# Logits of the stick-breaking attention: the queries' high by the keys' low parts as 64-row products, two query tiles issued as a pair

## The chip, the core and the metric

The kernel runs on one core of a Trainium2 chip. The metric is the device time of one execution in microseconds (us). The core has a matrix engine (TensorE, PE in the profile, whose weight loads are listed apart as PEld), a vector engine (DVE), a scalar engine (ACT), a general engine (POOL) and a queue that issues transfers (SP).

## What is computed

One layer of a gated encoder block: a combined input projection, an attention branch with 8 heads of 64 channels, a spatial gating branch, two up projections with gates, an output projection and a final norm. The change lies in the first line of the attention below.

```
def stick_breaking_attention(q, k, v):           # 1024 positions, 8 heads, 64 channels
    for start in range(0, s, Q_BLOCK):           # Q_BLOCK = 128
        z = einsum('bhqd,bhkd->bhqk', qb, kb)    # logits
        before = s_idx < t_idx
        log_keep = where(before, log_sigmoid(-z), 0.0)
        log_stick = cumsum(log_keep, reverse=True) - log_keep
        w = where(before, exp(log_sigmoid(z) + log_stick), 0.0)
        outs.append(einsum('bhqk,bhkd->bhqd', w, vb))
```

## The kernel before

Every float32 product is made of rounded parts: a value is split into a high part and a low part (`hi_lo`), both of type fp32r, and the products of the parts are added up in PSUM. The projections leave keys and queries of two heads at a time in DRAM, as `kq_hi[p]` and `kq_lo[p]`.

**One head.** `load_head(p, h)` brings four tiles of the tag `k` (6 buffers) to SBUF. A head has 64 channels and the array 128 rows, so `q` holds the high part of the queries in rows 0 to 63 and the low part in rows 64 to 127, while `kh` holds the keys' high part twice, one copy under the other, and `kl` the keys' low part twice. One product of `q` with `kh` over 128 rows is then high by high plus low by high, and one of `q` with `kl` is high by low plus low by low. `v` holds the values.

**One query tile.** `attn_row` works on 128 queries (tile `i`) by up to 512 keys (half `c`): both products go into one PSUM bank of the tag `z` (2 buffers), then ACT reads the bank twice (`keep` and `beta`, two sigmoids), a scan on DVE follows, and a product on DVE or POOL gives the weights. On the diagonal the tile is 128, 256, 384 or 512 keys wide, elsewhere 512. `attn_step` calls it for four tiles, transposes the weights on PE (bank `tr`) and multiplies them with the values (bank `o`). A head has 12 such query tiles, and 8 heads have 96: 16 each of 128, 256 and 384 keys, and 48 of 512.

**What sets the order.** The code doesn't issue anything itself. Each helper (`mm`, `act`, `load`, ...) records a task with an engine and a cost, and `Plan.issue` plays them through as a list scheduler: whenever an engine is free, it starts the recorded task with the lowest number of those that are ready and whose buffers can be had; a task that needs a buffer which is still held is passed over, and the next one in number is taken. `can_start` gives the buffers of a tag out in the order in which they were recorded. The program that results has a fixed order on each engine. The work of the projections (banks X, Y and Z) is recorded around the heads, and so stands between the products of the attention on PE.

```
for item in skipped:            # passed over: a buffer is held
    heapq.heappush(heap, item)
```

Of the kernel before, what the change touches and what calls it, by code (L numbers as in the profile page):

```python
# [10 lines left out]
F32 = mybir.dt.float32  # L11
F32R = mybir.dt.float32r
# [4 lines left out]
P = 128  # L17
S = 1024
# [72 lines left out]
class Plan:  # L91
# [10 lines left out]
    def buf(self, tag, shape=(P, 512), dt=F32):  # L102
        return Buf(self, tag, shape, dt)
# [22 lines left out]
        self.tasks.append(t)  # L126


    def mm(self, out, lhsT, rhs, start, stop, **kw):
        self.add("PE", max(0.109, rhs.n * 0.000417 + 0.0135) * (2 if rhs.buf.dt == F32 else 1),  # L130
                 lambda: self.nc.tensor.matmul(out.ap(), lhsT=lhsT.ap(), rhs=rhs.ap(), start=start, stop=stop, **kw),  # L131
                 [out], [lhsT, rhs])

# [200 lines left out]
def hybrid_block(  # L334
# [37 lines left out]
    pl = Plan(tc, make_tile, slots, psum_tags)  # L372
    buf = pl.buf
# [22 lines left out]
    def half_of(half):  # L396
        return slice(half * 512, half * 512 + 512)
# [201 lines left out]
    kq_hi = [buf("d", (2, P, S)) for _ in range(4)]  # L599
    kq_lo = [buf("d", (2, P, S)) for _ in range(4)]  # L600
# [33 lines left out]

    def load_head(p, h):
        hs = slice(64 * h, 64 * h + 64)
        kh, kl, q, v = (buf("k", (P, S), F32R), buf("k", (P, S), F32R), buf("k", (P, S), F32R),
                        buf("k", (P, 8, P), F32R))
        for side in range(2):
            pl.load(kh[64 * side:64 * side + 64, :], kq_hi[p][0, hs, :])  # L640
        pl.load(q[0:64, :], kq_hi[p][1, hs, :])
        pl.load(q[64:128, :], kq_lo[p][1, hs, :])
        for side in range(2):
            pl.load(kl[64 * side:64 * side + 64, :], kq_lo[p][0, hs, :])
        pl.load(v.all, v_all[:, :, 2 * p + h, :].map(lambda a: a.rearrange("b p c -> p b c")))
        return kh, kl, q, v
# [4 lines left out]
    nc.vector.memset(first_one.ap(), 0.0)  # L651
    nc.vector.tensor_copy(first_one.ap()[:, 384:512], ident.ap())

    def attn_row(kh, kl, q, i, c, cr):

        diag = i // 4 == c
        w = (i % 4 + 1) * P if diag else 512
        z = buf("z")[:, 0:w]
        qs, ks = q[:, i * P:(i + 1) * P], slice(512 * c, 512 * c + w)
        pl.mm(z, qs, kh[:, ks], True, False)  # L660
        pl.mm(z, qs, kl[:, ks], False, True)
        keep, beta = buf("ak", (P, 544)), buf("r")
        pl.act(keep[:, 0:w], z, AF.Sigmoid, scale=-0.125)
        pl.act(beta[:, 0:w], z, AF.Sigmoid, scale=0.125)
        edge = keep[:, w:w + 1]
        kr = keep[:, 0:w].map(lambda a: a[:, ::-1])
        if diag:
            pl.add("POOL", 0.15, lambda: nc.gpsimd.memset(edge.ap(), 0.0), [edge], [])
            pl.scan(kr, kr, first_one[:, 512 - w:512].map(lambda a: a[:, ::-1]), 0.0)
            if c == 1:  # L670
                pl.copy(cr, keep[:, 0:1])
        else:
            pl.copy(edge, cr)
            pl.scan_mult(kr, kr, cr)
        pl.tt(beta[:, 0:w], beta[:, 0:w], keep[:, 1:w + 1], ALU.mult, eng="DVE" if diag else "POOL")
        return beta

    def attn_step(kh, kl, q, v, p, h, ch, os_):
        o = buf("o")
        first = True  # L680
        for c in range(ch, -1, -1):
            crs = [carry[:, 8 * (2 * p + h) + ii:8 * (2 * p + h) + ii + 1] for ii in range(4)]
            w = [attn_row(kh, kl, q, 4 * ch + ii, c, crs[ii]) for ii in range(4)]
            for j in range(4):
                i0 = j if c == ch else 0
                off = i0 * P
                tr = buf("tr")
                for ii in range(i0, 4):
                    pl.transpose(tr[:, ii * P:(ii + 1) * P], w[ii][:, j * P:(j + 1) * P], ident)
                wh, wl = buf("e", dt=F32R), buf("e", dt=F32R)  # L690
                pl.hi_lo(wh[:, off:512], wl[:, off:512], tr[:, off:512])
                va = v[:, 4 * c + j, :]
                pl.mm(o[:, off:512], va, wh[:, off:512], first, False)
                pl.mm(o[:, off:512], va, wl[:, off:512], False, c == 0 and j == 3)
                first = False
        mine, other = slice(64 * h, 64 * h + 64), slice(64 - 64 * h, 128 - 64 * h)
        pl.copy(os_[mine, :], o[other, :])
        pl.tt(os_[mine, :], o[mine, :], os_[mine, :], ALU.add)
        if h == 1:
            g = buf("f1")  # L700
            pl.load(g.all, za[p][:, half_of(ch)])
            pl.tt(os_.all, os_.all, g.all, ALU.mult, eng="POOL")
            if p < 3:
                pl.store(y_a[p][:, half_of(ch)], os_.all)
# [119 lines left out]
    def head(p, h):  # L824
        parts = load_head(p, h)
        for ch in range(2):
            if h == 0:
                sums_of[p, ch] = buf("os")
            attn_step(*parts, p, h, ch, sums_of[p, ch])
# [4 lines left out]
    for word in ORDER.split():  # L834
        name = word.strip("+0123456789")
        n = int(word[-1])
# [115 lines left out]
    for c in range(2):  # L952
        for a in range(2):
            t = buf("T", (P, 4, 512))
# [81 lines left out]
```

## Time and profile before

| | |
|---|---|
| median of 3 runs | 761.28 us (761.17 to 762.08) |
| profiled execution, its own time | 762.38 us |
| its span, first to last instruction | 760.5 us |
| PE busy | 734.5 us, 97% |
| PEld busy | 607.9 us, 80% |
| DVE, ACT, POOL busy | 563.3, 432.2, 304.4 us |

Times in the rows are microseconds unless marked ns. A product on PE has two records, the load of its weights (PEld) and the product itself. Products follow one another before the record of the one ahead has ended, so what one costs on the engine is the distance from its start to the next one's start, not the length of its record; in a row that merges several of a kind, the first starts at the time shown, and the last ends at that time plus the length. L131 is the line of the helper `mm`, through which all products go, L135 that of the transposes; they are told apart by their tiles. `k,k` are the logits (a tile of keys and the tile of queries), `T,b` the projections, `e,k` the weights by values, `c,r` the transposes of the weights. A clock of 1.00 is the upper of the two levels of TensorE's clock, 2.4 GHz.

### The profile page before, as it was taken

To read this page: it belongs to the slowest core of one execution; us is meant where nothing else is said; L and a number is where in the kernel's file an instruction comes from. 1 tells how busy PE (TensorE), PEld (TensorE's weight loads), DVE (VectorE), ACT (ScalarE), POOL (GpSimd) and SP (SyncE) were. 2 spreads that over 40 slices of the span, in tenths; PEclk is the share of its full clock that TensorE was granted. 3 is DMA by queue.
4 is the path that set the end of the run, shared out by engine and by line. 5 is a ranking of instruction groups with operands and counts; after the bars stand their busy time and mean duration, and the time that the engine had idled before them with its cause. 6 is when DMAs were issued, how large, how long until landed. Compare 5 with 4: busy or idle time off the path is not lost.

```text
span 760.5 us, 10807 instructions
## 1 busy us (share of the span) xinstructions
PE 734.5 (97%) x3524; PEld 607.9 (80%) x3524; DVE 563.3 (74%) x788; ACT 432.2 (57%) x920; POOL 304.4 (40%) x298
## 2 busy tenths in 40 slices
PE   4998999999999999999999999999999999999996
PEld 3876888888888888878888788888888878888885
DVE  4769544688858877888979888798888999961132
ACT  6645754655746556657677585767856555431122
POOL 1400364598647963561655535260321140013110
PEclk9999999999999999999999999999999999999999
DMA  9513259633344554453656336464697837880022
GB/s 343 183 42 109 72 179 250 204 87 137 104 152 129 173 206 142 116 172 112 170 162 179 99 99 192 125 153 153 220 318 232 239 112 230 258 300 2 28 83 111
DMA packets 69177, 121.31 MB, mean 160 GB/s; under 512 B 7296, under 2 KB 17024, under 8 KB 69120
## 3 DMA queue, kind: packets, MB, share of 16 engines
q1 hardware_dynamic: 67968, 118.52, 50.1%
q10 hardware_dynamic: 1152, 2.10, 0.7%
q8 instruction: 28, 0.46, 0.2%
q14 instruction: 29, 0.24, 0.1%
HBM read 81.27 MB, written 39.32 MB: 159 GB/s over the span
## 4 chain that ended last, share of the span: by engine, by line
PE 85%; DVE 4%; issue 4%; DMA 2%; POOL 2%; ACT 1%; SPq 0%; POOLq 0%; DVEq 0%
PE Y L131 22%; PE X L131 22%; PE Z L131 19%; PE z L131 9%; PE o L131 8%; PE tr L135 5%; DVE T L168 1%; DMA k<-d 1%; DVE ak L192 1%; DMA k<-in_x_dram 1%; POOL a L168 1%; POOL r L168 1%; DMA f<-d 1%; DVE b L168 0%; POOL b L168 0%
## 5 line engine op out<-in xcount | busy, mean ns | idle before, releaser
L131 PE MATMUL Y<-T,b 128*128 128x512 f32 x672 | 182.7, 400 | 2.8 <-ACT b L159 2.0
L131 PE MATMUL X<-T,b 128*128 128x512 f32 x660 | 176.1, 397 | 0.0
L159 ACT CAST b<-a 128x512 fp32r<-128x512 f32 (+1 forms) x152 | 93.3, 616 | 103.3 <-PE X L131 25.1
L131 PE MATMUL Z<-T,b 128*128 128x512 f32 x540 | 145.2, 397 | 0.0
L131 PEld LDWEIGHTS Y<-T,b 128*128 128x128 f32 x672 | 123.0, 189 | 26.8 <-ACT b L159 2.4
L131 PEld LDWEIGHTS X<-T,b 128*128 128x128 f32 x660 | 120.7, 188 | 22.9 <-ACT Y L159 0.3
L168 DVE TENSOR_TENSOR b<-a,b 128x512 fp32r<-128x512 f32 (+1 forms) x112 | 100.2, 896 | 47.3 <-ACT b L159 42.1
L131 PEld LDWEIGHTS Z<-T,b 128*128 128x128 f32 x540 | 98.7, 189 | 18.9
L168 POOL TENSOR_TENSOR b<-a,b 128x512 fp32r<-128x512 f32 x40 | 58.3, 1457 | 104.4 <-ACT b L159 97.3
L168 POOL TENSOR_TENSOR f<-f,f 128x512 f32<-128x512 f32 (+1 forms) x38 | 59.1, 1563 | 37.3 <-ACT f L148 17.7
L168 POOL TENSOR_TENSOR a<-a,a 128x512 f32<-128x512 f32 x40 | 60.9, 1523 | 26.2 <-DVE b L168 21.5
L168 POOL TENSOR_TENSOR r<-r,ak 128x512 f32<-128x512 f32 x32 | 46.6, 1466 | 54.7 <-DVE ak L192 46.0
L199 DVE TENSOR_TENSOR_SCAN ak<-ak,c 128x128 f32<-128x128 f32 (+1 forms) x64 | 63.2, 990 | 4.2 <-ACT ak L148 4.0
L131 PE MATMUL o<-e,k 128*128 128x512 f32 (+1 forms) x192 | 59.6, 343 | 1.6 <-DVE e L168 1.5
L168 DVE TENSOR_TENSOR e<-tr,e 128x512 fp32r<-128x512 f32 (+1 forms) x96 | 52.1, 546 | 11.9 <-ACT e L159 11.3
L131 PE MATMUL z<-k,k 128*128 128x512 f32 (+2 forms) x216 | 60.2, 355 | 0.2 <-DMA k<-d 0.2
L135 PE MATMUL tr<-c,r 128*128 128x128 f32 x320 | 58.7, 273 | 1.0 <-POOL r L168 1.0
L148 ACT ACTIVATE ak<-z 128x128 f32<-128x128 f32 (+2 forms) x96 | 47.2, 494 | 20.1 <-PE z L131 14.5
L159 ACT CAST e<-tr 128x512 fp32r<-128x512 f32 (+1 forms) x96 | 45.7, 479 | 22.3 <-PE tr L135 19.7
L148 ACT ACTIVATE r<-z 128x128 f32<-128x128 f32 (+2 forms) x96 | 47.1, 494 | 14.3 <-PE tr L135 13.9
L192 DVE TENSOR_TENSOR_SCAN ak<-ak,c 128x512 f32<-128x512 f32 x32 | 50.6, 1594 | 0.0
L135 PEld LDWEIGHTS tr<-c,r 128*128 128x128 f32 x320 | 40.6, 140 | 12.3 <-POOL r L168 1.8
(217 smaller groups left out, 1144.9 us busy)
## 6 DMA issues: line engine op xcount, KB each, us to landing
d<-f SPq DMA_DIRECT2D x112, 256.0 KB, 2.8
a<-in_w_pairs_dram SPq DMA_DIRECT2D x80, 256.0 KB, 2.7
f<-d SPq DMA_DIRECT2D x72, 256.0 KB, 3.6
k<-d SPq DMA_DIRECT2D x48, 256.0 KB, 5.4
k<-in_x_dram SPq DMA_DIRECT2D x8, 512.0 KB, 7.2
d<-b SPq DMA_DIRECT2D x16, 256.0 KB, 2.3
k<-d SPq DMA_DIRECT2D x8, 512.0 KB, 6.9
a<-in_w_up_dram SPq DMA_DIRECT2D x16, 256.0 KB, 3.9
```

The lines of the kernel that those rows point to most:

```text
L131: lambda: self.nc.tensor.matmul(out.ap(), lhsT=lhsT.ap(), rhs=rhs.ap(), start=start, stop=stop, **kw),
L135: self.add("PE", 0.109, lambda: self.nc.tensor.transpose(out=out.ap(), in_=in_.ap(), identity=ident.ap()), [out], [in_, ident])
L148: return self.nc.scalar.activation(out=out.ap(), in_=in_.ap(), func=func, scale=sc, **kw)
L159: lambda: self.nc.scalar.copy(out=out.ap(), in_=in_.ap()), [out], [in_])
L168: self.add(eng, cost, lambda: e.tensor_tensor(out=out.ap(), in0=in0.ap(), in1=in1.ap(), op=op), [out], [in0, in1])
L192: lambda: self.nc.vector.tensor_tensor_scan(out.ap(), in_.ap(), in_.ap(), 1.0 if init is None else init.ap(), op0=ALU.mult, op1=ALU.bypass),
L199: lambda: self.nc.vector.tensor_tensor_scan(out.ap(), in_.ap(), floor.ap(), init, op0=ALU.mult, op1=ALU.max), [out], [in_, floor])
```

## The change

The products of `q` with `kl` are made over 64 rows of the array in place of 128: only the high part of the queries is multiplied with the low part of the keys, and low by low is left out. The query tiles are taken in pairs. In the odd tile of a pair the two parts of `q` are swapped, so that its high part lies in rows 64 to 127, and the product of the even tile uses rows 0 to 63, that of the odd tile rows 64 to 127. `logits` records, for a pair: even by `kh`, odd by `kh`, odd by `kl`, even by `kl`; the last has a planning cost of 0.03 us. `attn_row` no longer makes the products, and takes a bank.

To swap the parts, `q` gets the shape (128, 4, 2, 128) and is loaded by four transfers of 64 rows by 4 by 128 elements (pieces of 512 bytes), where there were two of 64 rows by 1024 elements (pieces of 4 KB).

```
-    def mm(self, out, lhsT, rhs, start, stop, **kw):
+    def mm(self, out, lhsT, rhs, start, stop, beside=False, **kw):
-        self.add("PE", max(0.109, rhs.n * 0.000417 + 0.0135) * (2 if rhs.buf.dt == F32 else 1),
+        self.add("PE", 0.03 if beside else max(0.109, rhs.n * 0.000417 + 0.0135) * (2 if rhs.buf.dt == F32 else 1),
...
-        kh, kl, q, v = (buf("k", (P, S), F32R), buf("k", (P, S), F32R), buf("k", (P, S), F32R),
+        kh, kl, q, v = (buf("k", (P, S), F32R), buf("k", (P, S), F32R), buf("k", (P, 4, 2, P), F32R),
...
-        pl.load(q[0:64, :], kq_hi[p][1, hs, :])
-        pl.load(q[64:128, :], kq_lo[p][1, hs, :])
+        for odd in range(2):
+            for side in range(2):
+                src = (kq_hi, kq_lo)[odd ^ side][p][1, hs, :]
+                pl.load(q[64 * side:64 * side + 64, :, odd, :],
+                        src.map(lambda a, odd=odd: a.rearrange("p (n t c) -> p n t c", t=2, c=P)[:, :, odd, :]))
...
+    def logits(kh, kl, q, i, c):
+        zs = []
+        for k in range(2):
+            w = ((i + k) % 4 + 1) * P if i // 4 == c else 512
+            zs.append(buf("z"))
+            pl.mm(zs[k][:, 0:w], q[:, i // 2, k, :], kh[:, 512 * c:512 * c + w], True, False)
+        for k in (1, 0):
+            w = ((i + k) % 4 + 1) * P if i // 4 == c else 512
+            rows = slice(64 * k, 64 * k + 64)
+            pl.mm(zs[k][:, 0:w], q[rows, i // 2, k, :], kl[rows, 512 * c:512 * c + w], False, True, beside=k == 0)
+        return zs
...
-        z = buf("z")[:, 0:w]
-        qs, ks = q[:, i * P:(i + 1) * P], slice(512 * c, 512 * c + w)
-        pl.mm(z, qs, kh[:, ks], True, False)
-        pl.mm(z, qs, kl[:, ks], False, True)
+        z = z[:, 0:w]
...
-            w = [attn_row(kh, kl, q, 4 * ch + ii, c, crs[ii]) for ii in range(4)]
+            w = []
+            for i2 in (0, 2):
+                zs = logits(kh, kl, q, 4 * ch + i2, c)
+                w += [attn_row(zs[k], 4 * ch + i2 + k, c, crs[i2 + k]) for k in range(2)]
```

What the planner makes of it on PE, in the second half of the first head's work. The names are: `z` the bank, `k_1089` the tile `kh`, `k_1111` the tile `q`, `k_1124` (after: `k_1125`) the tile `kl`; the size is that of the result, 128 queries by so many keys. Before:

```order
L131 MATMUL z_2942<-k_1089,k_1111 128x384
L131 MATMUL z_2942<-k_1124,k_1111 128x384
L131 MATMUL Y_2695<-T_684,b_2808 128x512
L131 MATMUL Y_2695<-T_704,b_2808 128x512
L131 MATMUL Y_2695<-T_684,b_2826 128x512
L131 MATMUL Y_2695<-T_684,b_2808 128x512
L131 MATMUL Y_2695<-T_704,b_2808 128x512
L135 MATMUL tr_2893<-c_66,r_2898 128x128
L135 MATMUL tr_2917<-c_66,r_2898 128x128
L131 MATMUL z_2965<-k_1089,k_1111 128x512
L131 MATMUL z_2965<-k_1124,k_1111 128x512
```

The same two query tiles, which are one pair, after:

```order
L132 MATMUL z_2952<-k_1089,k_1111 128x384
L132 MATMUL z_2952<-k_1125,k_1111 128x384
L132 MATMUL Y_2699<-T_684,b_2812 128x512
L132 MATMUL Y_2699<-T_704,b_2812 128x512
L132 MATMUL Y_2699<-T_684,b_2830 128x512
L132 MATMUL Y_2699<-T_684,b_2812 128x512
L132 MATMUL z_2963<-k_1089,k_1111 128x512
L132 MATMUL z_2963<-k_1125,k_1111 128x512
```

Each product with `kl` still stands right behind the product with `kh` of its own bank, and four products of a projection stand between the two tiles of the pair.

The place in the last head where two tiles of a pair come closest after the change (`k_5956` is `kh`, `k_6214` is `q`, `k_6387` is `kl`):

```order
L132 MATMUL z_6657<-k_5956,k_6214 128x512
L132 MATMUL z_6657<-k_6387,k_6214 128x512
L132 MATMUL z_6664<-k_5956,k_6214 128x512
L132 MATMUL z_6664<-k_6387,k_6214 128x512
L132 MATMUL o_6670<-e_6661,k_6417 128x512
```

Here too a product over 128 rows, the odd tile's with `kh`, stands between the two products over 64 rows.

On SP, the loads of the first head's `q` (`k_1111`) and `kl`, before:

```order
L224 DMA k_1089<-d_977 64x1024 x2
L224 DMA k_1111<-d_977 64x1024
L224 DMA a_1119<-in_w_spatial_dram 128x256
L224 DMA k_1124<-d_992 64x1024
L224 DMA k_1111<-d_992 64x1024
L224 DMA k_1124<-d_992 64x1024
```

and after:

```order
L225 DMA k_1089<-d_977 64x1024 x2
L225 DMA k_1111<-d_977 64x4x128 x2
L225 DMA a_1120<-in_w_spatial_dram 128x256
L225 DMA k_1125<-d_992 64x1024
L225 DMA k_1111<-d_992 64x4x128 x2
L225 DMA k_1125<-d_992 64x1024
```

The two transfers have become four, at the same place in the queue.

## Rows read from the trace of the kernel before

**Rows 1.** The page: busy time of each engine, and the granted clock in 40 slices.
```profile
PE 734.5 (97%) x3524; PEld 607.9 (80%) x3524; DVE 563.3 (74%) x788; ACT 432.2 (57%) x920; POOL 304.4 (40%) x298
PEclk9999999999999999999999999999999999999999
```

**Rows 2.** The page: the chain of work that ended last, by engine.
```profile
PE 85%; DVE 4%; issue 4%; DMA 2%; POOL 2%; ACT 1%; SPq 0%; POOLq 0%; DVEq 0%
```

**Rows 3.** Busy time by engine in the stretch of the heads (length, engines, clock, transfers).
```profile
core 0: us, PE busy (x) PEld busy (x) DVE busy (x) ACT busy (x) POOL busy (x), PEclk, DMA share, GB/s
288.00:618.00 330.00, 327.20 (x1640) 271.22 (x1639) 287.29 (x387) 220.18 (x517) 125.64 (x144) 1.00 0.58 171
```

**Rows 4.** Waits of PE in 285 to 625 us: total, times, longest.
```profile
PE o L131 <- DVE e L168: 1.5, 2, 1.1
PE tr L135 <- POOL r L168: 1.0, 2, 0.6
PE z L131 <- DMA k<-d: 0.2, 1, 0.2
```

**Rows 5.** Groups by line and form, PE and PEld: busy us, mean ns of one.
```profile
L131 PE MATMUL X<-T,b 128*128 128x512 f32 x660 | 176.1, 397 | 0.0
L131 PE MATMUL z<-k,k 128*128 128x512 f32 x120 | 38.4, 400 | 0.0
L131 PE MATMUL z<-k,k 128*128 128x384 f32 x32 | 8.2, 337 | 0.0
L131 PE MATMUL z<-k,k 128*128 128x128 f32 x32 | 6.9, 261 | 0.2 <-DMA k<-d 0.2
L131 PEld LDWEIGHTS z<-k,k 128*128 128x128 f32 x216 | 39.3, 188 | 7.7 <-DMA k<-d 0.6
```

**Rows 6.** PE in order of time, the first head: start, length, count.
```profile
288.55 0.60 PE L135 MATMUL z<-c,ak 128*128 128x128 f32 x4
288.91 0.42 PE L131 MATMUL z<-k,k 128*128 128x128 f32 x2
289.16 0.69 PE L131 MATMUL X<-T,b 128*128 128x512 f32 x2
...
292.22 0.51 PE L131 MATMUL z<-k,k 128*128 128x384 f32 x2
292.57 0.62 PE L131 MATMUL Y<-T,b 128*128 128x512 f32 x2
...
301.08 0.62 PE L131 MATMUL z<-k,k 128*128 128x512 f32 x2
301.53 1.07 PE L131 MATMUL X<-T,b 128*128 128x512 f32 x4
302.44 0.38 PE L135 MATMUL tr<-c,r 128*128 128x128 f32 x2
302.58 1.87 PE L131 MATMUL X<-T,b 128*128 128x512 f32 x7
304.29 0.39 PE L131 MATMUL o<-e,k 128*128 128x512 f32 x1
...
319.25 0.22 PE L131 MATMUL z<-k,k 128*128 128x128 f32 x1
319.31 2.51 PE L131 MATMUL Z<-T,b 128*128 128x512 f32 x10
```

**Rows 7.** The page: transfers into the tag k, KB each, median us to landing.
```profile
k<-d SPq DMA_DIRECT2D x48, 256.0 KB, 5.4
k<-d SPq DMA_DIRECT2D x8, 512.0 KB, 6.9
```

**Rows 8.** SP in order of time, loads of the third head.
```profile
346.16 1.09 SPq L224 DMA_DIRECT2D k<-d  x2
349.77 0.33 SPq L224 DMA_DIRECT2D a<-in_w_pairs_dram  x1
365.06 1.72 SPq L224 DMA_DIRECT2D k<-d  x3
```

**Rows 9.** PE in order of time, the third head's first product of logits.
```profile
367.37 0.22 PE L131 MATMUL z<-k,k 128*128 128x128 f32 x1
```

More of the change, by code (lines that the diff above doesn't have):

```diff
@@ L652, in hybrid_block, with attn_row @@
     nc.vector.tensor_copy(first_one.ap()[:, 384:512], ident.ap())
-    def attn_row(kh, kl, q, i, c, cr):
+    def logits(kh, kl, q, i, c):
[9 more added lines that the diff above has]
+        return zs
+    def attn_row(z, i, c, cr):
         diag = i // 4 == c
         w = (i % 4 + 1) * P if diag else 512
-        z = buf("z")[:, 0:w]
-        qs, ks = q[:, i * P:(i + 1) * P], slice(512 * c, 512 * c + w)
-        pl.mm(z, qs, kh[:, ks], True, False)
-        pl.mm(z, qs, kl[:, ks], False, True)
+        z = z[:, 0:w]
         keep, beta = buf("ak", (P, 544)), buf("r")
```

## The prediction

> **What bounds the kernel now.** I read the page's busy times and clock first, then the chain, then the stretch in which the heads are worked on, then who makes PE wait there, and last the single products. PE is busy 734.5 us of a span of 760.5, at a clock that stands at its upper level in every slice [rows 1], and 85% of the chain that ended last runs over PE [rows 2]. In the stretch of the heads, from 288 to 618 us, it is busy 327.20 of 330.00 us, and DVE, the next one, 287.29 [rows 3]. Between 285 and 625 us PE waited 2.7 us in all, of which 0.2 for the tiles that the change loads in another way [rows 4]. So in this stretch a microsecond more or less on PE is a microsecond of the whole. DVE has 43 us of room before it would become the bound.
>
> What a product costs PE is the distance between starts. The two products of a bank with 512 keys and what follows start at 301.08 and 301.53: 0.225 us each; with 384 keys 292.22 to 292.57, 0.175 each; a product of 128 keys between others 0.06 (319.25 to 319.31) [rows 6]. The record of a product of 512 lasts 0.397 us [rows 5], so it has a tail of about 0.17 us, in which the next one already runs.
>
> **What it would save, and what the order says of that.** The change wants the two products over 64 rows of a pair to run at the same time. There are 48 pairs: 16 of 128 beside 256 keys, 16 of 384 beside 512, 16 of 512 beside 512. If the narrower one vanished wholly, that would be 16 x (0.06 + 0.175 + 0.225) = 7.4 us, 1% of the time. But the order that the planner gives the changed program doesn't hold one such pair. Of the 96 products over 64 rows, none is next to another one. Each follows the product with `kh` of its own bank, or stands alone, and behind it comes a product over 128 rows. The reason is in the planner: the two banks `z` come free one after the other, since ACT has to read a bank twice before it is free. When the first one is free, the even tile's `kh` product starts, the odd tile's can't have its bank yet, and the lowest task that can run is the even tile's product with `kl`. Even where two tiles of a pair follow directly on one another, `kh` of the odd one lies between. PE executes this fixed order, so that the gain of 7.4 us can't arise; this is known before a run.
>
> The Trainium skill says in "TensorE: Matmul & The Clock Gate", Part 3, that products on different row groups run at the same time, a few nanoseconds apart. By it the pairs would give about what I worked out as the gain, if they were pairs; a product over 64 rows between two over 128 shares no time with either, as these use all rows.
>
> **What the change leaves and adds on PE.** The number of products and their columns stay: 3524 products, 96 of them now over 64 rows with the same 128 weights per row and the same up to 512 columns. Leaving out low by low takes rows, not columns, from the product, so I count nothing for it. New is that the array changes from 128 rows to 64 and back 96 times: 192 changes. The trace has no product over 64 rows, so it doesn't show their price; I bound it by neighbouring rows.
> - Lower end: nothing. The nearest change of kind in the trace is between products and transposes. Two transposes start at 302.44, seven products of 512 from 302.58, and the next one at 304.29 [rows 6]: 1.85 us, of which seven times 0.225 are 1.58, and two transposes at 0.11 (four at 288.55 in 0.60, a record being about 0.27) are 0.22. So 0.05 us is left for two changes of kind, 0.025 each. But there all 128 rows stay in use. A price below nothing I exclude: a product over 64 rows has the same number of columns, and neighbours over 128 rows leave it nothing to run beside.
> - Upper end: nothing of the next product may begin before the record of the one ahead has ended, and then its weights are loaded first: 0.397 + 0.188 - 0.225 = 0.36 us for a change [rows 5, 6]; 192 x 0.36 = 69 us.
> - Between: only the products themselves wait for one another, the weights are loaded beforehand. Then a change costs at most the tail, 0.17 us, and 192 x 0.17 = 33 us. It would be less if reading the next operand and writing the last result can lie over one another. Another row on a stall of this kind is the two products of 128 keys at 288.91, behind four transposes: with what follows at 289.16, 0.125 us each in place of 0.06, because weights are not loaded fast enough behind such short products [rows 6]; 0.065 each is what a partly hidden load costs.
>
> I take half of the tail, 0.08 us, which is near this last row: the last columns have to leave the array, but the read ahead and the write behind still overlap. 192 x 0.08 = 15.4 us.
>
> The Trainium skill has a rule that speaks against this change: "TensorEngine Tiling (Array Packing)", Tiling Modes, Key Properties, says that changing the tiling mode, and not only the tile, drains the engine. No row here shows it, and the page gives no price. An estimate by "TensorE: Matmul & The Clock Gate", Part 2, where the array drains in about 128 cycles: at 2.4 GHz that is 0.053 us, so 192 changes would be 10 us and the time 771.
>
> **The transfers.** `q` takes four transfers in place of two, 16 more in all, and of 512-byte pieces, 1024 for each head. The tile `v` is already loaded in 1024 such pieces: it lands 6.9 us after issue, where the other loads of the tag take 5.4 [rows 7]. SP's issue of two took 1.09 us [rows 8], so that 16 more are about 9 us on a queue that PE doesn't wait for. The cover: for the third head, the pair of loads at 346.16 is `q`, and the first product of that head starts at 367.37 [rows 8, 9], 21 us later; the four pieces need some 2.2 us of issue and 7 to land. The loads of `kl` stand behind them, but start 19 us later (365.06), when buffers come free. So I count nothing. If the cover were gone, a head would wait up to 1.5 us longer for its first product, 12 us over 8 heads; but PE has other products to do there.
>
> **The order otherwise.** Line by line the programs are similar: the same products, shifted by a few places against the projections. PE's own waits are 2.7 us in the stretch [rows 4], so that there is at most that to win, and I allow 3 us the other way. I count 0.
>
> **The sum.** The profiled execution took 762.4 us (span 760.5), 1.1 over the median of the runs. 762.4 + 15.4 = 777.8, and against the median 776.7. I predict 777 us.
>
> **The rivals.**
> - *Changing between 128 and 64 rows costs nothing.* Then only order and transfers are left, and the time is 759 to 764. For it: the change to transposes and back costs 0.025 us or less [rows 6]. Against it: there the array's division into rows stays the same, here sums have to leave it at another place. This is the rival on the other side, not slower; it decides if a change costs under 0.008 us (192 x 0.008 = 1.5 us). Chance 0.27.
> - *Weights wait too.* A product over other rows can't have its weights loaded while the one ahead runs. A change then costs 0.17 to 0.36 us, and the time is 794 to 830. For it: PEld is busy 607.9 us beside PE's 734.5 [rows 1], the kernel lives on loads that lie under products, and a load of 0.188 us that comes out from under a product of 0.225 nearly doubles it. Against it: it takes both costs at every one of 192 changes. Chance 0.25.
> - *The pairs do run side by side.* That would be 754. The order excludes it: chance 0.
>
> **How the numbers follow.** The forecast, a price of 0.03 to 0.17 us for a change, has 0.48 and gives 767 to 794. What a measurement of this kernel can tell from no change is about 0.2%, 1.5 us. Forecast and the second rival are slower throughout, 0.73; the first rival, spread over its range by the order's 3 us, gives faster 0.07, same 0.16, slower 0.04. So faster 0.07, same 0.16, slower 0.77. For the range I take the first rival whole (from 759), the forecast, and the second rival up to 812 (0.265 us for a change); what is left out is a good third of that rival, about 0.1, and some 0.05 below.
>
> **What the profile after would show.** Each step: the group of logits products splits in two, 96 over 64 rows; the number of PE's instructions stays 3524; the distance from a product over 64 rows to the next, and from the one ahead to it, is 0.03 to 0.17 us longer than 0.225; PE's busy time in the stretch of the heads grows by about 15 us, as the stretch itself does; the weight loads behind a change show whether they began before the product ahead ended (forecast) or after (second rival); no product over 64 rows starts within 0.1 us of another one. PE's waits for `k` stay under 1 us. I am wrong if the distances are 0.225 as before, if the stretch grows without them (then it is order or transfers), or if they are over 0.4.

## The result: slower by 5%, and the profile after

The changed kernel takes 801.64 us (801.54 to 801.72), the kernel before beside it 761.6 us: a ratio of 1.0514, 95% interval 1.0497 to 1.0531, 40 us more. The profiled execution has a span of 799.9 us, where it had 760.5.

The page after, busy times and clock, answers to [rows 1], and the chain to [rows 2]:

```profile
PE 773.6 (97%) x3524; PEld 609.7 (76%) x3524; DVE 560.5 (70%) x788; ACT 434.9 (54%) x920; POOL 299.5 (37%) x298
PEclk9999999999999999999999999999999998999998
...
PE 93%; DVE 2%; issue 2%; ACT 1%; DMA 1%; POOL 1%; SPq 0%; POOLq 0%; DVEq 0%; ACTq 0%
```

PE has the same 3524 products and is busy 39 us longer; the other engines do what they did. The weight loads take as long in sum (609.7 us, 607.9 before), so the loads as a whole did not get slower by themselves.

The groups of logits products by form (columns: busy us, mean ns of one, idle before), which answer to [rows 5]: the 64-row products have longer records than those over 128 rows, by 57 ns (128 keys) to 85 ns (512 keys).

```profile
L132 PE MATMUL z<-k,k 128*128 128x512 f32 x72 | 26.3, 411 | 0.0
L132 PE MATMUL z<-k,k 64*128 64x512 f32 x48 | 23.8, 496 | 0.0
L132 PE MATMUL z<-k,k 128*128 128x128 f32 x16 | 4.3, 267 | 0.0
L132 PE MATMUL z<-k,k 64*128 64x128 f32 x16 | 5.2, 324 | 0.0
```

Waits of the weight loads between 285 and 660 us (total us, times, longest) that the profile calls "issue", because it shows nothing that was waited for. The trace of before has none of them in its heads:

```profile
PEld z L132 <- issue: 26.3, 89, 0.4
PEld Z L132 <- issue: 4.5, 20, 0.2
PEld X L132 <- issue: 3.7, 16, 0.2
```

The second place where time went is the end of the last head. Busy time by engine in stretches around it:

```profile
core 0: us, PE busy (x) PEld busy (x) DVE busy (x) ACT busy (x) POOL busy (x), PEclk, DMA share, GB/s
288.00:630.00 342.00, 342.00 (x1544) 257.19 (x1543) 265.81 (x353) 206.74 (x474) 117.33 (x135) 1.00 0.53 160
...
645.00:662.00 17.00, 13.23 (x52) 7.93 (x51) 16.56 (x24) 13.38 (x37) 6.71 (x5) 0.92 0.05 16
662.00:670.00 8.00, 8.00 (x35) 6.71 (x34) 5.67 (x10) 1.80 (x3) 1.97 (x2) 0.75 0.16 57
```

From 288 to 630 us PE is busy all the time; before it was 327.20 of 330.00 [rows 3]. From 645 to 662 us it is busy 13.23 of 17 us, DVE 16.56: here DVE sets the pace. The granted clock falls within this stretch (0.92) and is 0.75 in the next one, so a part of each ran at the lower level, 1.2 GHz.

Set product against product by their number on PE, the changed kernel is 30.8 us late at the 2875th product (by then 89 of the 96 products over 64 rows have run), and 39.6 us at the 3125th, 63 us later; from there on nothing is added. So about 31 us come evenly over the heads and some 9 at the end of the last one.

### The profile page after: what moved, and what is told of

It is laid out like the page before. It is cut to its first block, busy times and chain, and to the rows that moved or that the text cites. A ratio compares the mean times of both kernels' runs of the same rounds, so it can differ in the third digit from the quotient of the medians.

```text
span 799.9 us, 10821 instructions
## 1 busy us (share of the span) xinstructions
PE 773.6 (97%) x3524; PEld 609.7 (76%) x3524; DVE 560.5 (70%) x788; ACT 434.9 (54%) x920; POOL 299.5 (37%) x298
## 4 chain that ended last, share of the span: by engine, by line
PE 93%; DVE 2%; issue 2%; ACT 1%; DMA 1%; POOL 1%; SPq 0%; POOLq 0%; DVEq 0%; ACTq 0%
PE Y L132 24%; PE X L132 23%; PE Z L132 20%; PE z L132 11%; PE o L132 9%; PE tr L136 5%; DMA k<-in_x_dram 1%; DVE T L169 1%; DVE ak L200 1%; PE z L136 0%; ACT T L160 0%; DVE f L169 0%; ACT ak L149 0%; POOL r L169 0%; POOL os L169 0%
## 5 line engine op out<-in xcount | busy, mean ns | idle before, releaser
L132 PE MATMUL Y<-T,b 128*128 128x512 f32 x672 | 184.7, 405 | 2.8 <-ACT b L160 2.0
L132 PE MATMUL z<-k,k 128*128 128x512 f32 (+2 forms) x216 | 76.6, 399 | 0.0
L169 POOL TENSOR_TENSOR f<-f,f 128x512 f32<-128x512 f32 (+1 forms) x38 | 56.0, 1483 | 35.1 <-ACT f L149 19.3
L132 PEld LDWEIGHTS z<-k,k 128*128 128x128 f32 x216 | 40.2, 186 | 32.0 <-issue 26.3
```

Source lines behind the costliest of these rows:

```text
L169: self.add(eng, cost, lambda: e.tensor_tensor(out=out.ap(), in0=in0.ap(), in1=in1.ap(), op=op), [out], [in0, in1])
```

## Experiments

**The rows alone.** The kernel before in its own order, engine by engine; only the 96 products with `kl` use 64 rows.

```
-        pl.mm(z, qs, kl[:, ks], False, True)
+        pl.mm(z, qs, kl[:, ks], False, True, rows=slice(0, 64))
```

`mm` then takes `lhsT.ap()[rows]` and `rhs.ap()[rows]`, while the planner sees whole tiles.

> The kernel before, in the same order on every engine and with its own loads; only the 96 products of q with kl use rows 0 to 63 in place of all 128, which leaves low by low out. Changes between 128 and 64 rows: 184. Theory 1, the price is at the change (the trace after gives 40 us over 192 changes, 0.21 us each): 184 x 0.21 = 39 us, about 800 us. Theory 2, the price comes from the new order, the pairs' hold on two banks and the loads in small pieces: about 762 us.

Measured: 792.8 us, ratio 1.0396 (1.0381 to 1.0412), 30.6 us more. This is theory 1 in kind, with 0.166 us for each of 184 changes in place of 0.21; theory 2 falls as the main cause. As the order is that of the kernel before, the same products can be laid side by side. PE of this kernel at the two products of the bank that start at 301.08 in [rows 6], and the weight loads of the same stretch:

```profile
304.11 0.82 PE L131 MATMUL z<-k,k 128*128 128x512 f32 x2
304.86 1.19 PE L131 MATMUL X<-T,b 128*128 128x512 f32 x4
305.89 0.38 PE L135 MATMUL tr<-c,r 128*128 128x128 f32 x2
...
303.89 0.19 PEld L131 LDWEIGHTS z<-k,k 128*128 128x128 f32 x1
304.44 0.18 PEld L131 LDWEIGHTS z<-k,k 64*128 64x128 f32 x1 [0.36 <-issue]
304.86 0.76 PEld L131 LDWEIGHTS X<-T,b 128*128 128x128 f32 x4 [0.24 <-issue]
```

In the trace of before the weight loads of that stretch are:

```profile
300.85 0.42 PEld L131 LDWEIGHTS z<-k,k 128*128 128x128 f32 x2
301.31 0.87 PEld L131 LDWEIGHTS X<-T,b 128*128 128x128 f32 x4
```

From the first product's start to the transposes 1.78 us pass (304.11 to 305.89), where 1.36 passed (301.08 to 302.44): 0.42 more for one product between two changes. Before, the second load began with the first product (300.85 + 0.42 - 0.19 = 301.08). Now it begins 0.33 us after the start of the product ahead (304.44), 0.1 later than that product's 0.225 us of columns, and the load behind it comes another 0.42 later (304.86). At each of the two changes 0.1 us passes in this way before the load begins; about 0.11 us more is lost at each, which I take for the part of the load of 0.18 us that the product has to wait for. This split is argued: the records of a load and of its product start together at a change. At none of the 184 changes in this trace does the load begin within the columns of the product ahead, so none is made in advance over a change of rows. Taken over all 96 places (start of the `kh` product to the start of the third one behind it, this kernel less the one before), the loss is 0.40 us for 512 keys, 0.39 for 384, 0.35 for 256 and 0.27 for 128, where the weights had been late already; together 35.1 us, of which 0.8 is counted twice where two of these places overlap. The 34.3 us left, 0.186 for a change, are what the changes cost on PE. Another 3.7 us PE got back outside of these places, nearly all of it at six where PE or its weight loads had waited for DVE or POOL in the kernel before, the largest just behind the stretch of [rows 4] (total us, times, longest):

```profile
PE Z L131 <- DVE T L168: 1.3, 1, 1.3
```

Of this wait 1.2 us are gone in the kernel with 64 rows.

**The order and the loads alone.** The changed kernel, in its own order on each engine, with 128 rows again.

```
+                  made_of=(q[:, i // 2, k, :], kl[:, 512 * c:512 * c + w]))
```

`made_of` is what the product is made of, while the planner sees the rows as before.

> The changed kernel in its own order on every engine and with its own loads; only the products of q with kl use all 128 rows again. So it holds what the change costs apart from the rows. The trace after shows 31 us lost evenly over the heads and 8.7 us more at the last head's end, where PE waits and its clock falls. If order and loads are the cause of that end: 765 to 771 us. If the end is a consequence of the slower products too, about 762 us.

Measured: 768.4 us, ratio 1.0078 (1.0057 to 1.0099), 6 us more. Its busy times at the same place of the program:

```profile
611.00:628.00 17.00, 11.48 (x54) 7.46 (x53) 16.56 (x25) 12.75 (x36) 5.12 (x5) 0.99 0.14 44
628.00:635.00 7.00, 6.85 (x31) 5.59 (x31) 5.59 (x9) 2.51 (x5) 3.65 (x3) 0.78 0.04 11
```

The same picture as after: DVE 16.56 of 17 us, PE idle 5.5 us, the clock lower behind it. Up to the 2875th product this kernel is even 2 us ahead of the one before; it is 6 us behind at the 3125th. So the end of the last head belongs to the order, not to the rows. The kernel before still has projections there (`Z<-T,T`, `X<-T,T`), which lie between its products of the last head:

```profile
616.07 0.94 PE L131 MATMUL Z<-T,T 128*128 128x512 f32 x3
616.85 0.62 PE L131 MATMUL z<-k,k 128*128 128x512 f32 x2
617.31 0.63 PE L131 MATMUL Z<-T,T 128*128 128x512 f32 x2
...
618.23 2.00 PE L131 MATMUL X<-T,T 128*128 128x512 f32 x8
```

In the changed order those that could run are used up earlier. In this run's trace no projection stands on PE between the first and the last of these rows:

```profile
611.01 0.40 PE L132 MATMUL Y<-T,T 128*128 128x512 f32 x1
...
617.77 0.68 PE L132 MATMUL o<-e,k 128*128 128x512 f32 x2 [1.30 <-DVE e L170]
...
628.89 0.79 PE L132 MATMUL Z<-T,T 128*128 128x512 f32 x1
```

**Loads in small pieces alone.** The kernel before, in the same order on PE, ACT and DVE, with `q` in four transfers.

```
-        pl.load(q[0:64, :], kq_hi[p][1, hs, :])
-        pl.load(q[64:128, :], kq_lo[p][1, hs, :])
+        for odd in range(2):
+            for side in range(2):
+                src = (kq_hi, kq_lo)[side][p][1, hs, :]
+                pl.load(q4[64 * side:64 * side + 64, :, odd, :],
+                        src.map(lambda a, odd=odd: a.rearrange("p (n t c) -> p n t c", t=2, c=P)[:, :, odd, :]))
```

> The kernel before, in the same order on PE, ACT and DVE and over 128 rows; only q is loaded by four transfers of 512-byte pieces in place of two of 4 KB. If the loads are covered, as the prediction has it: 762 us. If they cost something: up to 12 us more, with waits of PE for the tiles k.

Measured: 761.48 us, ratio 0.9989 (0.9977 to 1.0001): nothing. The transfers (KB each, median us to landing) and PE's wait for them:

```profile
k<-d SPq DMA_DIRECT2D x32, 128.0 KB, 3.2
...
PE z L131 <- DMA k<-d: 0.2, 1, 0.2
```

The smaller transfers land in 3.2 us in the median, earlier than the larger ones [rows 7], and PE waits 0.2 us, as before [rows 4]. For the third head the four start to be issued at 345.20, and its first product starts at 366.42, 21 us later, as before [rows 8, 9].

**The planner told the price.** The changed kernel, each product over 64 rows counted at its time plus 0.4 us.

```
-        self.add("PE", 0.03 if beside else max(0.109, rhs.n * 0.000417 + 0.0135) * (2 if rhs.buf.dt == F32 else 1),
+        self.add("PE", max(0.109, rhs.n * 0.000417 + 0.0135) * (2 if rhs.buf.dt == F32 else 1) + (0.4 if beside else 0),
...
-            pl.mm(zs[k][:, 0:w], q[rows, i // 2, k, :], kl[rows, 512 * c:512 * c + w], False, True, beside=k == 0)
+            pl.mm(zs[k][:, 0:w], q[rows, i // 2, k, :], kl[rows, 512 * c:512 * c + w], False, True, beside=True)
```

> The changed kernel, but the planner counts each product over 64 rows at its own time plus 0.4 us, in place of 0.03 us for the even tile; this gives another order (188 changes of rows). Theory 1 (0.16 to 0.2 us for each change): 31 us in the heads stay. If the 8.7 us at the last head's end come from a wrong picture of the time in the planner, they vanish: about 793 us; if not, about 801 us.

Measured: 792.45 us, ratio 1.0393 (1.0371 to 1.0416): the price of the rows stays, the end is gone.

```profile
288.00:630.00 342.00, 340.41 (x1561) 253.84 (x1560) 288.44 (x390) 228.12 (x527) 133.07 (x149) 1.00 0.47 142
630.00:662.00 32.00, 32.00 (x143) 26.50 (x142) 16.16 (x25) 5.73 (x10) 0.00 (x0) 1.00 0.91 315
```

The last head is done at 622 us here, within the first stretch, in which PE stood still for 1.6 us in all. Projections are left behind it, so that PE is busy 32.00 of 32 us in the second, at the upper level of the clock. The order differs everywhere, so this shows that an order made with other costs hasn't got the loss at the end, not that the 0.03 alone made it.

**Pairs that are pairs.** The two products over 64 rows of a pair become one task, issued one right behind the other; three versions in the same order on PE: on rows 64 to 127 and 0 to 63, both on rows 0 to 63, and both over all 128 rows.

```
+        pair = []
+        for k in (1, 0):
...
+            pair.append((zs[k][:, 0:w], q[:, i // 2, k, :], kl[:, 512 * c:512 * c + w], slice(64 * k, 64 * k + 64)))
+        pl.mm_pair(pair)
```

> The changed kernel, but the two products over 64 rows of a pair are one task of the planner, so that all 48 pairs stand next to one another; 96 changes between 128 and 64 rows. Theory 1 (price at the change, and products on different rows run at the same time): 96 x 0.21 = 20 us, less up to 7.4 us for running side by side, so 774 us; 782 if they don't run side by side. Rival, the price belongs to each product over 64 rows whatever stands next to it: 40 us, 794 to 802 us.

> As the joined pairs, in the same order on PE, but both products of a pair use rows 0 to 63 (the queries' parts aren't swapped), so that they can't run side by side; 96 changes. Theory 1: 20 us, 782 us, and slower than the joined pairs on different rows by what running side by side saves, up to 7.4 us. Rival (price for each product): about 802 us.

> As the joined pairs, in the same order on PE and with the same loads, but the products of q with kl use all 128 rows: no change of rows. Theory 1: 762 us, within 3. Theory 2 (order, banks and loads in small pieces): above 770 us.

Measured: different rows 776.2 us, ratio 1.0184 (1.0161 to 1.0207); the same rows 782.46, 1.0268 (1.0241 to 1.0295); all rows 767.37, 1.0076 (1.0053 to 1.0098). By these intervals each time is known to about 2 us, and a difference of two to about 3. PE and its weight loads at one pair, 512 beside 384 keys, first on different rows, then on the same rows (L139 is the pair's task; its row merges both products and carries the size of the first):

```profile
304.86 0.47 PE L132 MATMUL z<-k,k 128*128 128x512 f32 x1
305.27 0.49 PE L139 MATMUL z<-k,k 64*128 64x512 f32 x2
305.69 0.97 PE L132 MATMUL X<-T,b 128*128 128x512 f32 x3
...
305.26 0.18 PEld L139 LDWEIGHTS z<-k,k 64*128 64x128 f32 x2 [0.24 <-issue]
305.69 0.53 PEld L132 LDWEIGHTS X<-T,b 128*128 128x128 f32 x3 [0.24 <-issue]
```

```profile
303.35 0.48 PE L132 MATMUL z<-k,k 128*128 128x512 f32 x1
303.76 0.67 PE L139 MATMUL z<-k,k 64*128 64x512 f32 x2
304.36 0.96 PE L132 MATMUL X<-T,b 128*128 128x512 f32 x3
...
303.76 0.29 PEld L139 LDWEIGHTS z<-k,k 64*128 64x128 f32 x2 [0.24 <-issue]
304.36 0.53 PEld L132 LDWEIGHTS X<-T,b 128*128 128x128 f32 x3 [0.31 <-issue]
```

On different rows both products lie within the record of one, 0.49 us, and both loads within that of one, 0.18: they run at the same time, and the pair takes 0.42 us (305.27 to 305.69) in place of 0.60 (303.76 to 304.36). For the 16 pairs of 512 beside 512 keys it is 0.43 in place of 0.66 (medians, read product by product from the two traces). Over the kernel that is 782.46 - 776.2 = 6.3 us, of the 7.4 that I had worked out as the most. On the same rows, the second product needs no new change, and against all rows that leaves 782.46 - 767.37 = 15.1 us for 96 changes, 0.157 each, with as many products over 64 rows as the run of rows alone, which lost twice that over 184 changes. So the price belongs to the change, and the rival that it belongs to the product falls. The version over all rows loses 5 us for its order, more than I had allowed. Counted product by product in the profiled execution, 4.3 us of it come between the 2875th and the 3125th, at the end of the last head.

## Why the prediction was right or wrong

- **Slower, and PE as the bound: right.** In the heads PE is busy throughout, and a loss on it is one of the whole, but for the 3.7 us that it got back where it had waited (34.3 us lost in the run of rows alone, 30.6 measured).
- **No pair runs side by side: right,** and read from the order alone. The 7.4 us that it would save at most were right in size too (6.3 in the joined pairs).
- **The price of a change: the step that failed.** I took 0.08 us, half of a product's tail, on the ground that "only the products themselves wait for one another, the weights are loaded beforehand". They are not. Where a product of 512 keys has clean neighbours (other products of 512 columns, over 128 rows), two changes cost 0.42 us: the load begins 0.1 us after the columns of the product ahead, and what is left is best explained by the product waiting for its load. Over the kernel it is 30.6 us for 184 changes and 15.1 for 96, 0.16 for a change, twice what I took (0.186 before what PE got back). A sign that I had named shows it too: the distance from a product over 64 rows with 512 keys to the next is 0.42 us, just over the 0.4 at which I was to be wrong. My second rival, "weights wait too", came nearer, but not whole. By it a load can't run while the product ahead does; at all 94 changes behind a product of 512 columns in the run of rows alone, the load begins 0.07 us before the record of that product ends (the profile models these ends). I had held against it that it would take both costs at every change; a change does take a part of both, 0.21 us beside clean neighbours, where both whole are 0.36. Its time, 794 to 830, holds the result in part by luck: the rows alone give 792.8, and the rest is the end of the last head, which it did not have. I gave it 0.25. That the kernel lives on loads which lie under products [rows 1] should have weighed more than the row of two short products [rows 6], where a load is late but was begun in advance.
- **The rule of the Trainium skill.** In "TensorEngine Tiling (Array Packing)", Tiling Modes, Key Properties, the Trainium skill says that changing the tiling mode drains the engine. These traces agree as far as they go: beside clean neighbours 0.1 us passes before the next load begins; that this is a drain, no trace shows. My estimate from the Trainium skill, "TensorE: Matmul & The Clock Gate", Part 2, 0.053 us for a drain, was too low as a price: it is half of that first part and a quarter of the 0.21 us in all.
- **The transfers cost nothing: right** (0.9989), with the cover that I had named.
- **The order costs nothing, 3 us at most: wrong.** It costs 6 us by itself: 8 are lost at the end of the last head, 2 won before it. In the changed kernel the end costs some 9. I had read the waits and DVE's room over the whole stretch; there DVE has 43 us of room [rows 3], at its end it has half a microsecond in 17. What the fall of the clock there adds was not separated.
- **The sum:** I had 15.4 us for the rows and 0 for the order. The two runs that separate them give 30.6 and 6, some 3 short of the 40. In the changed kernel's own order, rows against no rows is 801.64 - 768.4 = 33 us, as PE had next to no waits there to get anything back from (0.4 us up to the 2875th product of the kernel with 128 rows). Up to the 2875th product the rows cost 32.9 us there (30.8 late with them, 2.0 ahead without), 0.185 for each of 178 changes, as in the order before; at the end of the last head, where PE waits in any case, they add 0.8 us to the 8 of the order. My range, to 812, reached the time with a price twice too low and an order that I had at nothing; 777 was off by 25 us.

## What to carry to other kernels

Before a change that wants two instructions next to one another, look where the scheduler puts them: here two banks that come free one after the other pulled every pair apart, and only a joint task kept them together. On an engine that is kept full by loads made in advance, price a change of mode by what it takes from under cover, not by the pipeline's tail alone. Read an engine's room in the last microseconds of a stage too, where the filling work runs out.

## What was not expected of the hardware

A product over 64 rows between two over 128 costs 0.40 us more than one over 128 rows in the mean of the 48 places with 512 keys (0.42 at the one shown); two of them on different halves run wholly at the same time, loads and all (0.49 us for both records). By these rows a pair pays some 0.4 us for its two changes and saves 0.18 with 512 beside 384 keys (0.60 less 0.42), 0.23 with 512 beside 512 (0.66 less 0.43). So, as an estimate, two pairs of the wider kind between two changes would about break even, and of the other kind it would take three; that needs more banks than the two of `z`, and wasn't tried. No version here beats the kernel before. After a stretch of 17 us in which PE was busy 13.23, its granted clock was 0.75 over the next 8 us; in the kernel with 128 rows in the same order, after 11.48 of 17 us, it was 0.78 over the next 7.
